# A two-layer hybrid decoder trunk: the first layer's input also given transposed, its first two projections taken over all token blocks at once

## Chip, core and metric

One core of a Trainium2 chip runs the whole program. The metric is the device time of one execution in microseconds (us); lower is better. Engines are named as the profile names them: PE (TensorE matmuls), PEld (its weight loads), DVE (VectorE), ACT (ScalarE), POOL (GpSimd), SP (SyncE, which here only issues DMAs).

## What is computed

A trunk of two layers on 512 tokens of width 2048. Each layer normalises its input, projects it to 5952 columns, runs three groups of attention heads on the result, gates them, projects back and adds the residual. Cut to what bears on the change:

```python
def hybrid_layer(x, cos, sin, layer, pre_w, post_w, w_in, ...):
    h = rms_norm(x, pre_w)
    proj = h @ w_in
    a_q, a_k, a_v, a_g, b_q, b_k, b_v, b_g, c_q, c_kv, c_kr, c_g = jnp.split(proj, offsets, axis=-1)
    ...
    qb = apply_rope(b_q.reshape(B, S, SW_HEADS, SW_HEAD_DIM), cos4, sin4)
    kb = apply_rope(b_k.reshape(B, S, SW_KV_HEADS, SW_HEAD_DIM), cos4, sin4)
    vb = b_v.reshape(B, S, SW_KV_HEADS, SW_HEAD_DIM)
    y_b = sliding_window_attention(qb, kb, vb, sinks)
    ...
    return x + rms_norm(out, post_w)
```

The row scale of the norm, one over the root mean square of a token's row, commutes with the product, so the kernel multiplies the raw `x * pre_w` with `w_in` and puts the row scale on afterwards.

## The kernel before

**Products.** Every float32 operand is split into a rounded high part and a low remainder (`split`, L148: ACT writes the high part, DVE or POOL subtracts it). A product is three matmuls, high by high, high by low, low by high (`three`, L299), so each weight tile passes ACT (`whi`) and then DVE or POOL (`wlo`; even tiles DVE, odd ones POOL). `stream` (L279) loads two weight tiles of 128 rows in one DMA into one of three `raw` buffers; four `whi` and four `wlo` buffers let the splits run at most four tiles ahead of PE. `sweep` (L306) runs over the 16 tiles of a contraction: the first two tiles are taken together, block by block, and so are the last two (`tail=2`). Results lie in four PSUM banks `g`.

**Opening of a layer.** `act_hi` and `act_lo` hold the split input transposed, 16 tiles of 128 rows by 512 tokens. In layer 0 `load` (L1016) fetches `x` in pieces of 128 tokens by 512 columns; `feed` (L510) transposes four 128x128 squares of a piece on PE into a bank `hT`, DVE multiplies it by `pre_norm_w` into `h` (L526), and the split follows. ACT also squares each piece and sums along its row (L540); from these sums `row_scales` makes the row scales `r_in`, and `scaled_tables` (L269) multiplies the rotary tables by them.

The tokens are taken in two halves of two blocks (the loop `for half in range(2)`, L600). Each half sweeps the 320 columns of the keys and values (`C_KR` and `B_K`), then rotates them on DVE (`rope`, L233) into `kd`, then sweeps the 512 columns of the first eight query heads (`B_Q`) and rotates those into `q_rot`. A sweep of two blocks uses two of the four banks, so each weight tile is loaded and split twice, once for either half. `key_half` later transposes `kd` on PE (`kT`). The angle tables of the rotation are computed on DVE at the very start (`rope_tables`, L193), some 40 small instructions.

Then follow sweeps over all 512 tokens: the gates (`gate_chunk`, whose matmuls the rows call `g<-act_hi,whi`, with the activations named first), the other eight query heads, and so on.

**Order.** PE runs in the order in which the program is written. Small pieces of attention work wait in two lanes (`Lanes`), from which `sweep` draws one step after each group of tiles; a step may ask to be left for some microseconds. The other engines' order is set by a scheduler when the program is built; `late` pins an instruction to the written order. Each engine runs its own list strictly in order. SP issues all loads of weights and of `x`.

Of the kernel before, what the change touches and what calls it, by code (L numbers as in the profile page):

```python
# [19 lines left out]
P = 128  # L20
# [88 lines left out]
def trunk(ctx: ExitStack, tc: tile.TileContext, ins, inv_freq, out):  # L109
# [83 lines left out]
    def rope_tables():  # L193
        pos_i = sm("pos_i", NB, I32)
        freq = slot("freq", "et", shape=(P, 32))
        nc.gpsimd.dma_start(out=pos_i, in_=ins["positions"].rearrange("b (m p) -> p (b m)", p=P))
        nc.gpsimd.dma_start(out=freq, in_=inv_freq.partition_broadcast(P))
        co, si = tabs
        pos = sm("pos", NB)
        V.tensor_copy(pos, pos_i)  # L200
        H = 32 * NB
        room = [slot("angles", "rot") for _ in range(2)]
        ang, r, t, *ks = (room[i // 4][:, H * (i % 4):H * (i % 4) + H] for i in range(6))
        for m in range(NB):
            V.tensor_scalar(ang[:, 32 * m:32 * m + 32], freq, pos[:, m:m + 1], None, op0=ALU.mult)
        pc = two_pi_pieces()
        V.tensor_copy(r, ang)
        for k, e in zip(ks, (22, 11, 0)):
            V.tensor_scalar(t, r, 1.0 / (2 * math.pi * 2.0 ** e), MAGIC, op0=ALU.mult, op1=ALU.add)
            V.tensor_scalar(k, t, -MAGIC, None, op0=ALU.add)  # L210
            if e:
                for j in range(3):
                    V.scalar_tensor_tensor(r, k, -pc[j] * 2.0 ** e, r, op0=ALU.mult, op1=ALU.add)
        V.tensor_copy(r, ang)
        for lev, j in ((0, 0), (1, 0), (0, 1), (2, 0), (1, 1), (0, 2), (2, 1), (1, 2), (0, 3), (2, 2)):
            V.scalar_tensor_tensor(r, ks[lev], -pc[j] * 2.0 ** (22, 11, 0)[lev], r,
                                   op0=ALU.mult, op1=ALU.add)
        V.tensor_scalar(t, r, 1.0 / (2 * math.pi), MAGIC, op0=ALU.mult, op1=ALU.add)
# [8 lines left out]
        rv, tv = (z.rearrange("p (m f) -> p m f", f=32) for z in (r, t))  # L227
        A.activation(co[:, :, 0:32], tv, AF.Sin)
# [47 lines left out]

    ahead, behind, fine, last_rows = [False], [True], [False], [False]

    def stream(w, segs, nk, C, rows=0, before=None):  # L279

        for k0 in range(0, nk, 2):
            raw = wraw.tile([P, 2, S], F32, name="raw", tag="raw")
            c = 0
            for off, width in segs:
                nc.sync.dma_start(
                    out=raw[:, :, c:c + width],
                    in_=w[rows + k0 * P:rows + (k0 + 2) * P, off:off + width].rearrange("(k p) c -> p k c", p=P))
# [17 lines left out]

    def sweep(tiles, nk, jobs, after=None, tail=2):  # L306

# [34 lines left out]

    def gemm_tok(block, w, segs, C, nk=KT, ms=range(NB), kruns=None, before=None, tail=2):
# [8 lines left out]
        sweep(tiles(), nk, [lambda t, a, z, p=p, m=m: three(p[:, 0:C], block(t[0], m), t[1:], a, z)  # L352
                            for p, m in zip(ps, ms)], tail=tail)
        return ps
# [112 lines left out]

    def column(name, l, n):

        t = layer_c.tile([P, n], F32, name=f"{name}{l}")  # L470
        if l == 0:
            nc.scalar.dma_start(out=t, in_=ins[name][l].rearrange("(k p) -> p k", p=P))
        else:
            late(nc.sync.dma_start(out=t, in_=ins[name][l].rearrange("(k p) -> p k", p=P)))
        return t

    def layer_constants(l):
        c = dict(qnw=column("mla_q_norm_w", l, 4), kvnw=column("mla_kv_norm_w", l, 4))
        lam_init = 0.8 - 0.6 * math.exp(-0.3 * l)
        sub = layer_c.tile([P, 1], F32, name=f"sub{l}")  # L480
        late(nc.sync.dma_start(out=sub, in_=ins["diff_subln_w"][l].rearrange("(p o) -> p o", o=1)))
        V.tensor_scalar(sub, sub, 0.5 * (1.0 - lam_init), None, op0=ALU.mult)
        sink = layer_c.tile([P, 16], F32, name=f"sink{l}")
# [25 lines left out]

    def feed(half, xs, pre, r_in, there, first=False):  # L510

# [4 lines left out]
        def turn(lane, u):  # L516
            c = slice(u * P, u * P + P)
            for n in range(4):
# [4 lines left out]
                for j in range(4):  # L523
# [4 lines left out]
                                op=ALU.mult)  # L528
                split(act_hi[:, half, 4 * n:4 * n + 4, c], act_lo[:, half, 4 * n:4 * n + 4, c], h,
                      E=nc.gpsimd if first and u else V)  # L530
                done[u] += 1
            yield L_FEED2

        def scale(lane):
            yield L_SCALE
            ssps = [sm("ssp") for _ in range(2)]
            for n in range(4):
                for u in range(2):
                    sq = slot("sq", f"qE{lane}")
                    late(A.activation(sq, xs[n][u], AF.Square, accum_out=ssps[u][:, n:n + 1]), first)  # L540
                yield L_FEED2
# [13 lines left out]
    def layer(l, pre, norms, r_in, start=None):  # L555
# [16 lines left out]
        def fed(half, k):  # L572
            if start and half == 0:
                start(k)
            tasks, done, _ = norms[half]
# [23 lines left out]
        keys = []  # L599
        for half in range(2):  # L600
            ms = (2 * half, 2 * half + 1)
            ps = gemm_tok(act_block, w_in, [(C_KR, 64), (B_K, 256)], 320, ms=ms,
                          before=lambda k: fed(half, k))
            lanes.finish(norms[half][2])
            scaled_tables(r_in, half, rtabs)
            lanes.finish(*keys)
            kd = []
            for t_ps, m in zip(ps, ms):
                d = slot("kd", "rot")
# [5 lines left out]
            keys.append(lanes.add(key_half, half, kd))  # L615
            if half == 0:
                c = layer_constants(l)
            ps = gemm_tok(act_block, w_in, [(B_Q, 512)], 512, ms=ms)
# [32 lines left out]

        def sw_pair(lane, g, pr):
            qq = stack_q(lane, f"qE{lane}", qt[g], 128 * pr)
            yield L_SPLIT
# [301 lines left out]
        post = norm_rows("post_norm_w", l, "k")  # L956
        nxt = None if final else column("pre_norm_w", l + 1, KT)
        ssp = [sm("ssp") for _ in range(NB)]
# [49 lines left out]
    r_in = layer_c.tile([P, NB], F32, name="r_in0")  # L1008
    norms = []

    pre = column("pre_norm_w", 0, KT)
    loads = [(half, n) for half in range(2) for n in range(4)]
    xs = [[[None] * 2 for _ in range(4)] for _ in range(2)]
    there = [[0], [0]]

    def load():  # L1016
        half, n = loads.pop(0)
        for u in range(2):
            m = 2 * half + u
            xs[half][n][u] = slot("x0", "gy")  # L1020
            late(nc.sync.dma_start(out=xs[half][n][u], in_=ins["x"][0, m * P:(m + 1) * P, n * S:(n + 1) * S]))
        there[half][0] += 1
        if n == 0:
            norms.append(feed(half, xs[half], pre, r_in, there[half], half == 0))

    def start(k):
        if loads and k % 2 == 0:
            load()

    rope_tables()  # L1030
    for _ in range(N_LOAD):
        load()
    state = layer(0, pre, norms, r_in, start)
# [13 lines left out]
L_DA = 4.5  # L1047
N_LOAD = 2
L_KEYS = 5.0
# [27 lines left out]
```

## Time and profile before

| | us |
|---|---|
| median of 3 runs | 1787.97 (1786.29 to 1790.8) |
| the profiled execution, its own time | 1790.11 |
| its span in the profile | 1788.3 |
| PE busy in the span | 1732.1 (97%), 8832 matmuls |
| DVE, ACT, POOL busy | 917.7 (51%), 820.1 (46%), 765.6 (43%) |
| DMA | 202.25 MB, mean 113 GB/s |

The profile divides the span into 40 slices of 44.7 us. PE's busy share is six tenths in the first slice, eight in the second and nine or more in nearly all others. A timeline lists instructions by start and duration; matmuls are pipelined, so the time between two starts, and not the duration, is what one costs.

### The profile page before, as it was taken

The page shows a single profiled execution, that of the slowest core. Times are in us where ns is not written, and L with a number is a line of the kernel's source. Part 1 is how long each engine was busy: PE and PEld are TensorE (multiplying, and loading weights), DVE is VectorE, ACT ScalarE, POOL GpSimd, SP SyncE. Part 2 cuts the span into 40 slices and gives each one's busy share as a digit, 9 for nine tenths or more (in the row PEclk, how much of TensorE's full clock was granted, in tenths as well). Part 3 has the DMA queues.
Part 4 walks back from the last instruction along what each step waited for, and adds up shares of the span by engine and source line. Part 5 has one row for each costly group of instructions (what it writes and reads, how often), then busy time and mean ns, then how long its engine had stood idle before and what let it go on. Part 6 is the DMA issues. An engine that isn't in the chain of part 4 may idle for free. (4 is left out here: it accounts for less than half of the span.)

```text
span 1788.3 us, 25313 instructions
## 1 busy us (share of the span) xinstructions
PE 1732.1 (97%) x8832; PEld 1488.4 (83%) x8832; DVE 917.7 (51%) x2246; ACT 820.1 (46%) x1792; POOL 765.6 (43%) x650
## 2 busy tenths in 40 slices
PE   6899999999999999999988999999999999999997
PEld 5778888888899998888777888888889999888885
DVE  7755516654336658301776555256534357672035
ACT  5555525544344545325554454255444444452353
POOL 4343343443434344448344444433434434444550
PEclk9999999999999999999999999999999999999999
DMA  7452232232323233325765422322323222332366
GB/s 196 133 158 77 83 101 83 83 88 78 109 74 84 71 97 110 118 95 186 238 190 151 118 88 83 95 83 67 104 77 104 81 74 75 114 121 96 115 205 221
DMA packets 168671, 202.25 MB, mean 113 GB/s; under 512 B 30800, under 2 KB 92256, under 8 KB 168544
## 3 DMA queue, kind: packets, MB, share of 16 engines
q1 hardware_dynamic: 162160, 190.12, 35.9%
q0 software_dynamic: 3264, 10.51, 1.6%
q8 instruction: 69, 1.13, 0.3%
q10 hardware_dynamic: 3120, 0.01, 0.1%
q14 instruction: 58, 0.48, 0.1%
HBM read 188.02 MB, written 12.58 MB: 112 GB/s over the span
## 5 line engine op out<-in xcount | busy, mean ns | idle before, releaser
L152 POOL TENSOR_TENSOR wlo<-raw,whi 128x512 fp32r<-128x512 f32 (+2 forms) x592 | 734.9, 1248 | 930.2 <-ACT whi L151 899.6
L151 ACT CAST whi<-raw 128x512 fp32r<-128x512 f32 (+3 forms) x704 | 406.0, 581 | 635.4 <-PE g L142 489.5
L142 PE MATMUL g<-wlo,act_hi 128*128 128x512 f32 (+2 forms) x1408 | 522.9, 371 | 26.8 <-DVE wlo L152 23.8
L142 PE MATMUL g<-whi,act_hi 128*128 128x512 f32 (+2 forms) x1408 | 526.9, 374 | 4.1 <-ACT whi L151 4.1
L142 PE MATMUL g<-whi,act_lo 128*128 128x512 f32 (+2 forms) x1408 | 519.5, 369 | 0.6 <-POOL act_lo L152 0.6
L142 PEld LDWEIGHTS g<-wlo,act_hi 128*128 128x128 f32 x1408 | 267.9, 190 | 71.1 <-DVE wlo L152 31.7
L142 PE MATMUL g<-act_hi,whi 128*128 128x512 f32 x768 | 310.9, 405 | 0.6 <-DVE vl L155 0.6
L142 PE MATMUL g<-act_hi,wlo 128*128 128x512 f32 x768 | 303.6, 395 | 0.0
L142 PE MATMUL g<-act_lo,whi 128*128 128x512 f32 x768 | 303.4, 395 | 0.0
L142 PEld LDWEIGHTS g<-whi,act_hi 128*128 128x128 f32 x1408 | 268.0, 190 | 40.0 <-ACT whi L151 5.7
L142 PEld LDWEIGHTS g<-whi,act_lo 128*128 128x128 f32 x1408 | 267.8, 190 | 35.1 <-POOL act_lo L152 0.9
L142 PEld LDWEIGHTS g<-act_hi,wlo 128*128 128x128 f32 x768 | 144.3, 188 | 34.6
L142 PEld LDWEIGHTS g<-act_hi,whi 128*128 128x128 f32 x768 | 144.6, 188 | 30.4 <-DVE vl L155 1.5
L142 PEld LDWEIGHTS g<-act_lo,whi 128*128 128x128 f32 x768 | 144.7, 188 | 29.1
L152 DVE TENSOR_TENSOR wlo<-raw,whi 128x512 fp32r<-128x512 f32 (+1 forms) x112 | 79.0, 711 | 96.0 <-ACT whi L151 95.9
L152 DVE TENSOR_TENSOR pTl<-pT,pTh 128x512 fp32r<-128x512 f32 (+2 forms) x112 | 68.2, 612 | 99.7 <-ACT pTh L151 99.6
L968 DVE TENSOR_TENSOR ob<-g,post_norm_w 128x512 f32<-128x512 f32 x32 | 22.1, 690 | 176.8 <-ACT sq L966 176.7
L151 ACT CAST pTh<-pT 128x512 fp32r<-128x512 f32 (+2 forms) x112 | 58.6, 525 | 45.4 <-PE pT L146 44.6
L436 DVE CUSTOM_DVE_ANT_0 p<-sc,causal 128x128 f32<-128x128 f32 (+3 forms) x96 | 46.0, 480 | 33.1 <-PE sc L142 33.1
L146 PE MATMUL pT<-ident,p 128*128 128x128 f32 x384 | 61.0, 274 | 1.4 <-DVE p L833 1.4
L644 ACT ACTIVATE p<-p,nm 128x256 f32<-128x256 f32 (+1 forms) x128 | 59.9, 469 | 0.0
L438 ACT ACTIVATE p<-p,nm 128x128 f32<-128x128 f32 (+3 forms) x64 | 36.0, 562 | 51.4 <-DVE nm L437 51.4
(236 smaller groups left out, 2042.6 us busy)
## 6 DMA issues: line engine op xcount, KB each, us to landing
raw<-w_in SPq DMA_DIRECT2D x144, 512.0 KB, 3.6
raw<-w_out SPq DMA_DIRECT2D x96, 512.0 KB, 3.8
raw<-w_in SPq DMA_DIRECT2D x192, 128.0 KB, 2.4
raw<-w_in SPq DMA_DIRECT2D x32, 256.0 KB, 3.1
x<-x SPq DMA_DIRECT2D x16, 256.0 KB, 4.8
y_spill<-gate POOLq DMA_DIRECT2D x16, 256.0 KB, 3.0
raw<-w_ukv SPq DMA_DIRECT2D x8, 512.0 KB, 3.8
yb<-y_spill POOLq DMA_DIRECT2D x16, 256.0 KB, 4.0
```

Of the source, the lines that this page charges most:

```text
L142: nc.tensor.matmul(out_, a, b, start=start, stop=stop, skip_group_check=True)
L146: nc.tensor.transpose(out_, in_, ident)
L151: late(A.copy(hi, src), behind)
L152: E.tensor_tensor(lo, src, hi.bitcast(F32), op=ALU.subtract)
L436: V.tensor_tensor_reduce(p, scores, mask, 1.0, -3e38, op0=ALU.add, op1=ALU.max, accum_out=mx)
L438: A.activation(p, p, AF.Exp, bias=nm, scale=scale, accum_out=den)
L644: A.activation(blocks[i], blocks[i], AF.Exp, bias=nm[:, i:i + 1], scale=64.0 ** -0.5, accum_out=den[:, i:i + 1])
L968: V.tensor_tensor(ob[n][m], t, post[n], op=ALU.mult)
```

## The change

The host writes two more inputs: `x_t`, the transposed input as 16 tiles of 128 rows by 512 tokens, and `cols`, the per-column norm weights with one row of 25 numbers per partition (before, they were fetched as single numbers by several DMAs). In layer 0:

- there are no transposes and no `hT`, `h`: `take` splits a tile of `x_t` straight into `act_hi` and `act_lo`, with `pre_norm_w` as the scale of both instructions;
- the squares are taken of the transposed tiles (`square`), added tile by tile on DVE into `ssum`, and PE sums over the partitions (`col_sums`, tile `css`) in a lane task, `first_scale`, which is added at step 13 of the first sweep;
- the first sweep is the queries' (512 columns) for all four blocks, without the pairing of its first two tiles (`head=False`); the scaled tables and the rotation of the four query blocks follow; the second sweep is the keys' and values' (320 columns) for all four blocks, with `tail=3`;
- `rope_tables` is cut into pieces that are written between the steps of the first sweep;
- the very first weight load is two DMAs of one tile each; the residual is still read from `x`.

Layer 1 keeps its halves; only its column weights come from `cols`.

```diff
-            if n == 0 or nk - tail <= n < nk - 1:
+            if (n == 0 and head) or nk - tail <= n < nk - 1:
...
+        kv_segs = [(C_KR, 64), (B_K, 256)]
+        if start:
+            ps = gemm_tok(act_block, w_in, [(B_Q, 512)], 512, before=start, head=False)
+            lanes.finish(*norms)
+            for half in range(2):
+                scaled_tables(r_in, half, rtabs)
+            for m in range(NB):
+                qt[0][m] = rotate_q(ps[m], m)
+            c = layer_constants(l, pre)
+            kd = key_tiles(gemm_tok(act_block, w_in, kv_segs, 320, tail=3), range(NB), None)
+            keys += [lanes.add(key_half, half, kd[2 * half:2 * half + 2]) for half in range(2)]
+        for half in range(0 if start else 2):
...
+    def take(k):
+        x = xt[k].rearrange("p (h t) -> p h t", h=2)
+        split(act_hi[:, :, k, :], act_lo[:, :, k, :], x, pre[:, k:k + 1], behind=k < 4)
...
+        late(A.activation(sq, xt[k], AF.Square))
+        if k:
+            V.tensor_tensor(ssum, ssum, sq, op=ALU.add)
+        if k == KT - 1:
+            norms.append(lanes.add(first_scale))
+
+    def first_scale(lane):
+        yield L_FIRST
+        ms = sm("ms")
+        V.tensor_scalar(ms, col_sums(bank("css", lane), ssum), 1.0 / DM, EPS, op0=ALU.mult, op1=ALU.add)
+        V.tensor_copy(r_in, rsqrt(ms, "rin"))
+        yield 0.0
...
+    def start(k):
+        while loaded[0] < min(2 * k + 3, k + N_LOAD, KT):
+            load(loaded[0])
+            loaded[0] += 1
+        while taken[0] < min(k + 1 if k < 2 else 2 * k, k + N_TAKE, KT):
+            take(taken[0])
+            taken[0] += 1
+        for _ in range(2):
+            if squared[0] < min(2 * (k - 3), taken[0]):
+                square()
...
+N_LOAD = 6
+N_TAKE = 3
+L_FIRST = 2.0
```

**PE, from the first sweep to the second, in the changed kernel.** `g_135` is the fourth bank of the queries' sweep, `g_632` the first of the keys'; the two share no name but the pool has four banks, so `g_632` takes the place of the queries' first bank.

```order
L142 MATMUL g_135<-whi_534,act_hi_88 128x512
L142 MATMUL g_135<-wlo_535,act_hi_88 128x512
L142 MATMUL g_135<-whi_534,act_lo_89 128x512
L142 MATMUL css_563<-ones_f_91,ssum_115 128x2 x4
L142 MATMUL g_632<-whi_639,act_hi_88 128x320
L142 MATMUL g_632<-wlo_640,act_hi_88 128x320
```

The sums `css` stand behind the last matmul of the queries' sweep and right ahead of the keys' first one; before, the row sums came from ACT, and PE had no part in them.

**DVE at the same place in the changed kernel** (`ms` is the mean square, `rsq_u` and `rin` the steps of its inverse root, `rcos` and `rsin` the scaled tables, L249 to L259 the rotation).

```order
L1058 TENSOR_SCALAR ms<-css 128x4
L160 TENSOR_SCALAR rsq_u<-ms 128x4
...
L1059 COPY r_in_112<-rin 128x4
L281 TENSOR_TENSOR rcos<-cos,r_in_112 128x128
...
L249 TENSOR_TENSOR rope<-g,rsin 128x8x32
L251 TENSOR_TENSOR rope<-g,rsin 128x8x32
L253 TENSOR_TENSOR q_rot<-g,rcos 128x512
L249 TENSOR_TENSOR rope<-g,rsin 128x8x32
L259 TENSOR_TENSOR q_rot<-q_rot,rope 128x512
```

From `ms` to `r_in` stand 13 instructions, then four of the tables, then four rotations of four instructions each, with the fourth of a rotation one place later, behind the first of the next.

**DVE within the first sweep, before:**

```order
L526 TENSOR_TENSOR h_269<-hT_264,pre_norm_w0_113 128x512
L213 SCALAR_TENSOR_TENSOR angles_121<-angles_122,angles_121 128x128
L526 TENSOR_TENSOR h_278<-hT_273,pre_norm_w0_113 128x512
L209 TENSOR_SCALAR angles_121<-angles_121 128x128
L526 TENSOR_TENSOR h_297<-hT_292,pre_norm_w0_113 128x512
```

**and in the change:**

```order
L219 SCALAR_TENSOR_TENSOR angles_169<-angles_169 128x128
L152 TENSOR_TENSOR wlo_397<-raw_380,whi_396 128x512
L219 SCALAR_TENSOR_TENSOR angles_169<-angles_170,angles_169 128x128
L155 SCALAR_TENSOR_TENSOR act_lo_89<-xt_313,cols0_113,act_hi_88 128x2x256
L219 SCALAR_TENSOR_TENSOR angles_169<-angles_170,angles_169 128x128
L1051 TENSOR_TENSOR ssum_115<-ssum_115,sq_416 128x512
```

Ahead of `ms` DVE now has 16 instructions on `act_lo`, 15 on `ssum`, 8 on the queries' `wlo` and about 42 small ones, mixed like this; the `h` instructions, which read PSUM, are gone.

## Rows read from the trace of the kernel before

Rows of stretches give the stretch and its length, then busy time and number of instructions of PE, PEld, DVE, ACT and POOL, then the granted clock, the DMA share and GB/s. Rows of a timeline give start, duration, engine, line, operation and tiles.

**Rows 1.** Busy time by engine in one stretch, the opening up to the gates:

```profile
0.00:115.00 115.00, 92.34 (x462) 78.06 (x463) 78.73 (x189) 62.98 (x140) 48.15 (x53) 0.96 0.61 171
```

**Rows 2.** What PE waited for in the first 115 us (total, times, longest):

```profile
PE g L142 <- DVE wlo L152: 12.9, 8, 5.5
```

**Rows 3.** Timeline of PE, steady matmuls of both widths, and the gates' first:

```profile
84.75 0.31 PE L142 MATMUL g<-wlo,act_hi 128*128 128x320 f32 x1
...
89.73 0.31 PE L142 MATMUL g<-whi,act_lo 128*128 128x320 f32 x1
...
104.72 0.40 PE L142 MATMUL g<-whi,act_lo 128*128 128x512 f32 x1
...
114.52 0.40 PE L142 MATMUL g<-whi,act_lo 128*128 128x512 f32 x1
114.75 0.40 PE L142 MATMUL g<-act_hi,whi 128*128 128x512 f32 x1
```

**Rows 4.** Timeline of PE after its longest wait in the opening:

```profile
28.41 0.64 PE L142 MATMUL g<-wlo,act_hi 128*128 128x320 f32 x1 [5.54 <-DVE wlo L152]
28.85 0.47 PE L142 MATMUL g<-whi,act_lo 128*128 128x320 f32 x1
29.12 0.47 PE L142 MATMUL g<-whi,act_hi 128*128 128x320 f32 x1
...
32.58 0.40 PE L142 MATMUL g<-wlo,act_hi 128*128 128x320 f32 x1
```

**Rows 5.** Timeline of the first 10 us: loads of x, first transposes, first product:

```profile
0.74 1.81 SPq L1021 DMA_DIRECT2D x<-x  x4
...
4.28 1.09 PE L146 MATMUL hT<-ident,x 128*128 128x128 f32 x4 [4.28 <-DMA x<-x]
...
10.07 0.64 PE L142 MATMUL g<-whi,act_hi 128*128 128x320 f32 x1 [3.01 <-ACT whi L151]
```

**Rows 6.** Busy time in two stretches of 5 us, for the DMA rate (last column):

```profile
0.00:5.00 5.00, 0.72 (x4) 0.72 (x4) 0.00 (x0) 0.37 (x1) 3.59 (x14) 1.00 0.56 105
...
15.00:20.00 5.00, 5.00 (x39) 4.86 (x37) 4.28 (x12) 2.37 (x6) 1.47 (x2) 1.00 1.08 363
```

**Rows 7.** Timeline of DVE: small and wide passes, each with its successor:

```profile
28.29 0.28 DVE L216 SCALAR_TENSOR_TENSOR angles<-angles 128x128 f32<-128x128 f32 x1
28.49 0.48 DVE L152 TENSOR_TENSOR wlo<-raw,whi 128x320 fp32r<-128x320 f32 x1
...
43.38 0.68 DVE L152 TENSOR_TENSOR act_lo<-h,act_hi 128x512 fp32r<-128x512 f32 x1
43.98 0.15 DVE L165 SCALAR_TENSOR_TENSOR rin<-rsq_u,rin 128x2 f32<-128x2 f32 x1
```

**Rows 8.** Timeline of POOL and DVE side by side:

```profile
24.08 2.13 POOL L152 TENSOR_TENSOR wlo<-raw,whi 128x320 fp32r<-128x320 f32 x2
24.13 1.36 DVE L152 TENSOR_TENSOR act_lo<-h,act_hi 128x512 fp32r<-128x512 f32 x1
...
52.32 1.29 POOL L152 TENSOR_TENSOR wlo<-raw,whi 128x512 fp32r<-128x512 f32 x1 [3.91 <-ACT whi L151]
```

**Rows 9.** Timeline: column sums on PE and the inverse root on DVE, later in layer 0:

```profile
378.97 0.95 PE L142 MATMUL css<-ones_f,ssum 128*128 128x2 f32 x8
...
379.96 0.16 DVE L739 TENSOR_TENSOR ms<-css,r_sq 128x4 f32<-128x4 f32 x1 [9.22 <-PE css L142]
...
382.54 0.16 DVE L741 SCALAR_TENSOR_TENSOR qscale<-rlat,r_in 128x4 f32<-128x4 f32 x1
```

**Rows 10.** Timeline of DVE: a scaled table, and the rotation of one query block:

```profile
46.01 0.28 DVE L274 TENSOR_TENSOR rcos<-cos,r_in 128x128 f32<-128x128 f32 x1
...
71.98 0.41 DVE L242 TENSOR_TENSOR rope<-g,rsin 128x256 f32<-128x256 f32 x1
72.31 0.41 DVE L244 TENSOR_TENSOR rope<-g,rsin 128x256 f32<-128x256 f32 x1
72.64 0.68 DVE L246 TENSOR_TENSOR q_rot<-g,rcos 128x512 f32<-128x512 f32 x1
```

More of the change, by code (lines that the diff above doesn't have):

```diff
@@ L274, in scaled_tables @@
             V.tensor_tensor(dst[:, mm_, :], src[:, mm_, :], rb, op=ALU.mult)
-    ahead, behind, fine, last_rows = [False], [True], [False], [False]
+    ahead, behind, fine, last_rows, opening = [False], [True], [False], [False], [True]
     def stream(w, segs, nk, C, rows=0, before=None):
@@ L284, in stream @@
             for off, width in segs:
-                nc.sync.dma_start(
-                    out=raw[:, :, c:c + width],
-                    in_=w[rows + k0 * P:rows + (k0 + 2) * P, off:off + width].rearrange("(k p) c -> p k c", p=P))
+                for j, n in ((0, 1), (1, 1)) if opening[0] else ((0, 2),):
+                    nc.sync.dma_start(
+                        out=raw[:, j:j + n, c:c + width],
+                        in_=w[rows + (k0 + j) * P:rows + (k0 + j + n) * P, off:off + width].rearrange(
+                            "(k p) c -> p k c", p=P))
+                opening[0] = False
                 c += width
@@ L304, in three, with sweep @@
         mm(out_ap, al, bh, start=False, stop=last)
-    def sweep(tiles, nk, jobs, after=None, tail=2):
+    def sweep(tiles, nk, jobs, after=None, tail=2, head=True):
         def run(group):
@@ L341, in gbanks, with gemm_tok @@
         return [psg.tile([P, S], F32, name="g", tag="g") for _ in range(n)]
-    def gemm_tok(block, w, segs, C, nk=KT, ms=range(NB), kruns=None, before=None, tail=2):
+    def gemm_tok(block, w, segs, C, nk=KT, ms=range(NB), kruns=None, before=None, tail=2, head=True):
         ps = gbanks(len(ms))
@@ L465, in spread, with columns, layer_constants @@
         mm(t, ones_r, diag[1], start=False, stop=True)
[L468 to L474, printed above, removed]
[L475 to L478 removed]
+    def columns(l):
+        t = layer_c.tile([P, KT + 9], F32, name=f"cols{l}")
+        late((nc.sync if l else nc.scalar).dma_start(out=t, in_=ins["cols"][l]), l > 0)
+        return t
+    def layer_constants(l, cols):
+        c = dict(qnw=cols[:, KT:KT + 4], kvnw=cols[:, KT + 4:KT + 8])
         lam_init = 0.8 - 0.6 * math.exp(-0.3 * l)
         sub = layer_c.tile([P, 1], F32, name=f"sub{l}")
[L481 to L482 removed]
+        V.tensor_scalar(sub, cols[:, KT + 8:KT + 9], 0.5 * (1.0 - lam_init), None, op0=ALU.mult)
         sink = layer_c.tile([P, 16], F32, name=f"sink{l}")
@@ L508, in row_scales, with feed @@
         return rsqrt(ss, name, n)
-    def feed(half, xs, pre, r_in, there, first=False):
+    def feed(half, xs, pre, r_in, there):
         done = [0, 0]
@@ L528, in turn @@
                                 op=ALU.mult)
-                split(act_hi[:, half, 4 * n:4 * n + 4, c], act_lo[:, half, 4 * n:4 * n + 4, c], h,
-                      E=nc.gpsimd if first and u else V)
+                split(act_hi[:, half, 4 * n:4 * n + 4, c], act_lo[:, half, 4 * n:4 * n + 4, c], h)
                 done[u] += 1
@@ L599, in layer, with key_tiles @@
         keys = []
[L600 to L606, printed above, removed]
+        def key_tiles(ps, ms, tag):
             kd = []
             for t_ps, m in zip(ps, ms):
-                d = slot("kd", "rot")
+                d = slot("kd", tag or f"p{m % 2}")
                 rope(d[:, 0:384], t_ps[:, 0:192], m, 3, rtabs, dup=3)
@@ L614, in layer @@
                           r_in[:, m:m + 1])
-            keys.append(lanes.add(key_half, half, kd))
+            return kd
+        kv_segs = [(C_KR, 64), (B_K, 256)]
[10 more added lines that the diff above has]
+        for half in range(0 if start else 2):
+            ms = (2 * half, 2 * half + 1)
+            ps = gemm_tok(act_block, w_in, kv_segs, 320, ms=ms, before=lambda k: fed(half, k))
+            lanes.finish(norms[half][2])
+            scaled_tables(r_in, half, rtabs)
+            lanes.finish(*keys)
+            keys.append(lanes.add(key_half, half, key_tiles(ps, ms, "rot")))
             if half == 0:
-                c = layer_constants(l)
+                c = layer_constants(l, pre)
             ps = gemm_tok(act_block, w_in, [(B_Q, 512)], 512, ms=ms)
@@ L652, in sw_pair @@
         def sw_pair(lane, g, pr):
+            if not all(t["done"] for t in keys):
+                yield lambda: all(t["done"] for t in keys)
             qq = stack_q(lane, f"qE{lane}", qt[g], 128 * pr)
@@ L956, in layer @@
         post = norm_rows("post_norm_w", l, "k")
-        nxt = None if final else column("pre_norm_w", l + 1, KT)
+        nxt = None if final else columns(l + 1)
         ssp = [sm("ssp") for _ in range(NB)]
@@ L1009, in trunk, with load, square @@
     norms = []
[L1011 to L1024, printed above, removed]
-    def start(k):
[L1027 to L1032, printed above, removed]
+    pre = columns(0)
+    xt, ssum = [None] * KT, slot("ssum", "raw")
+    pieces = rope_tables()
+    def load(k):
+        xt[k] = slot("xt", "gy")
+        late(nc.sync.dma_start(out=xt[k], in_=ins["x_t"][:, k, :]))
+    def take(k):
+        x = xt[k].rearrange("p (h t) -> p h t", h=2)
+        split(act_hi[:, :, k, :], act_lo[:, :, k, :], x, pre[:, k:k + 1], behind=k < 4)
+    loaded, taken, squared = [1], [0], [0]
+    def square():
+        k = squared[0]
+        squared[0] += 1
+        sq = slot("sq", f"qE{k % 2}") if k else ssum
+        late(A.activation(sq, xt[k], AF.Square))
[9 more added lines that the diff above has]
+        yield 0.0
+    def start(k):
+        while loaded[0] < min(2 * k + 3, k + N_LOAD, KT):
[7 more added lines that the diff above has]
+                square()
+        behind[0] = k < 3
+        if k:
+            next(pieces, None)
+    next(pieces)
+    load(0)
     state = layer(0, pre, norms, r_in, start)
@@ L1047 @@
 L_DA = 4.5
-N_LOAD = 2
+N_LOAD = 6
+N_TAKE = 3
+L_FIRST = 2.0
 L_KEYS = 5.0
```

20 lines of the change are left out of this document (16 added, 4 removed).

## The prediction

> **What bounds the kernel now.** The page comes first: PE is busy 97% of the span, the other engines about half of it, so PE's own order sets the time, except where PE waits. Next come the stretches. The opening, up to the gates' first matmul at 114.75 us [rows 3], holds only 92.3 us of busy PE in 115 [rows 1]; nearly all that this change can reach lies there. Then the waits of PE: the largest is for DVE's low parts of the weights, 12.9 us in 8 times, one of them 5.5 us [rows 2]. DVE is the busiest of the helpers there, 78.7 us [rows 1], so the opening is bound by DVE in its first part and by PE in its last.
>
> What PE must do in the opening is small. From 84.75 to 89.73 us lie 34 steps between matmuls of 320 columns, 0.1465 us each; from 104.72 to 114.52 lie 42 of 512 columns, 0.2333 us each [rows 3]. The two projections are 4 blocks by 16 tiles by 3, 192 matmuls of either width: 44.8 us for the queries and 28.1 us for the keys and values, 72.9 us of 114.75. The rest is transposes, waits, and a slow clock.
>
> **What the change removes.** 64 transposes leave PE. The sixteen wide `h` passes leave DVE. Every weight tile of the two projections is split once instead of twice, so 32 of 64 splits go. Fifteen wide `ssum` sums and the 13 instructions of one inverse root come instead of two such chains. I build the new opening as a sum of clock times and compare its end, the gates' first matmul, with 114.75.
>
> **1. First matmul: 6.3 us.** The first piece of `x` is there at 4.28 [rows 5]; the first tile of `x_t` is as large and first in SP's queue. Then a high part, the weights' high part and a low part follow one another, each a wide pass of 0.6 to 0.7 us [rows 7]: 4.28 + 3 x 0.65 = 6.2, taken as 6.3. Bounds: 4.9 (one pass, the rest beside it) and 10.07, where the first product starts now [rows 5].
>
> **2. Slow clock at the start: 2.3 us.** PE after its long idle ran a 320-column step in 0.27 us instead of 0.1465, from 28.41 to 32.58 us, 4.2 us long [rows 4]; that is the 1.2 GHz level beside the 2.4 GHz one. At 6.3 us PE has done nothing, so the first 12 matmuls of 512 columns cost about 0.427 each instead of 0.233: 12 x 0.194 = 2.3 us. Bounds 0 and 4.6, twice that.
>
> **3. The queries' sweep: 44.8 us, and 1.6 us of waits.** DVE has to keep pace. Until the last low part of this sweep it has 39 wide passes (16 `act_lo`, 15 `ssum`, 8 `wlo`), a wide pass releasing its successor after 0.60 us, and about 42 small ones at 0.2 us [rows 7], 0.22 with their dependences: 23.4 + 9.2 = 32.6 us, less than PE's 44.8. But a wide DVE pass with both operands in SBUF, started beside a POOL subtraction, took 1.36 us instead of 0.68 [rows 8]. POOL has 8 subtractions of 512 columns here, 1.29 us each [rows 8]; they would add 10.3 us to DVE if each blocked it in full: 42.9. It starts at about 5 and waits some 2 us for its first tiles, so it ends at 49.9; PE needs that low part two tiles (24 matmuls, 5.6 us) ahead of its own end at 6.3 + 2.3 + 44.8 = 53.4, at 47.8. The wait is thus 0 to 2.1 us; 1.6 is taken, since nearly every wide pass now has both operands in SBUF. The sweep ends at 55.0. The Trainium skill, "SBUF — State Buffer", section "Who interferes with whom", says that a VectorE instruction with two SBUF inputs and a GpSimd one that reads SBUF exclude each other for a whole instruction. The trace agrees (1.36 for 0.68). By that rule in its full form the wait is 2.1 us and the time 0.5 us longer; without it, 0 and 1.6 us shorter.
>
> **4. From the queries to the keys: 9.3 us lost.** This is what the change adds. All four banks hold query results, and PE's next matmul needs the first of them. `css` stands behind the sweep's last matmul, so the whole chain to the row scale starts there. PE's sums to `ms`: 378.97 to 379.96, 1.0 us; from `ms` over 13 steps to the last: 2.6 us [rows 9]. Four table products, started every 0.2 us, by their 0.28 us duration: 0.9 [rows 7, 10]. The first block's three PSUM reads start 0.33 and 0.33 apart and the third, a wide pass, frees the bank 0.60 after its start [rows 7]: 1.26 [rows 10]. With 0.4 for a POOL subtraction in the way [rows 8], PE goes on 1.0 + 2.6 + 0.9 + 1.3 + 0.4 = 6.2 us after the sweep. Each later block costs DVE four instructions, 0.33 + 0.33 + 0.60 + 0.60 = 1.86 us, so the fourth bank is free at 6.2 + 5.6 = 11.8. Between them PE has six matmuls a block, 0.9 us at full clock and 1.6 at half, which [rows 4] an idle time of 6 us brings; both fit into 1.86. After the last six, at 12.8, PE has done 24 matmuls worth 3.5: 9.3 us lost. Bounds: 7 (tables and POOL beside the chain) and 13 (slow clock for 4 us afterwards, and every DVE pass held up).
>
> **5. The keys' sweep: 28.1 us.** Its splits take half the columns per PE time of before and DVE has little else. **6. On to the gates: 0.3 us.** The keys' rotation reads at most 320 columns of a bank, so no block costs more than 1.86 us against 1.3 us (9 x 0.1465) of PE's last group per block; at the most 4 x 0.56 = 2.2 us. **7. Later: 1.2 us.** The 12 transposes of the keys, before within the opening, now come among the gates' matmuls, at under the 0.1465 of a 320-column step: at most 1.8, taken as 1.2.
>
> Sum: 6.3 + 2.3 + 44.8 + 1.6 + 9.3 + 28.1 + 0.3 + 1.2 = 93.9 us against 114.75: **20.8 us saved**. Behind it PE runs without a gap, so the start of all that follows moves by as much. The single tidier column loads of layer 1 I cost at nothing: SP has slack there, and if it had none they would be worth under 1 us. The profiled execution took 1790.11, which is 2.1 above the median of 1787.97; 1790.11 - 20.8 = 1769.3, against the median 1767.2 us.
>
> **Rivals.** (a) *DVE bounds the opening.* If the POOL exclusion also lengthens POOL, whose delayed odd tiles hold PE, and each small step waits for its predecessor, DVE gets 39 x 0.68 + 42 x 0.32 + 10.3 = 50.3 us instead of 42.9: 7.4 us more before the first matmul of the last group, most of it PE's. Saved 13 to 14, 1774 us. For it: DVE bounds the opening now [rows 2]. Against: the small steps are mixed with wide ones, which hides their dependences. (b) *The gain is given back.* The keys are transposed later, so the sliding-window tasks in the lanes start later; if their first four had to be waited for, PE would idle. It would end within 5 us of 1788. Against: in the order their last matmuls still stand 12 tiles of 12 matmuls ahead of the point that needs them (20 before), 12 x 12 x 0.233 = 33 us. (c) *Slower: the loads starve the opening.* The first sweep needs 4.2 MB of `x_t` and 4.2 MB of weights within the first 50 us. At 105 GB/s, as in the first 5 us, 8.4 MB take 80 us, the sweep ends at about 82, and the opening takes 121 us: 1794 us. It decides below 8.4 MB in 55 + 20.8 = 76 us, 111 GB/s. Against: 363 GB/s flowed from 15 to 20 us [rows 6], in the same 2 KB lines. (d) *The clock stays low.* The four short bursts of step 4 are too thin to bring the clock back, and the keys' sweep runs its first 4.2 us at half speed, as after the 5.5 us gap [rows 4]: 2.1 us more, with the last burst's 0.7 some 2.8, 1770 us. For it: PE is busy 4 x 0.9 of 12.8 us. Against: at half clock the bursts last 1.6 of each 1.86 us, nearly without a gap. The Trainium skill, "TensorE: Matmul & The Clock Gate", section "HAM oscillation — how this bites in real kernels", describes PE falling back to the cold clock in each of many waits; that speaks for (d), and the trace shows it for one long gap (0.27 us for 0.1465).
>
> **How the numbers follow.** About 0.3%, 5.4 us, is what a measurement of this kernel can tell from no change. The forecast, the sum of the steps, has 0.63, (a) 0.24, (b) 0.05, (c) 0.03, (d) 0.05. The forecast alone spans 1761 to 1772: the favourable bounds (first matmul 1.4 earlier, no DVE wait, 7 instead of 9.3) save 26 us, the unfavourable ones (3.7 later by step 4, some more cold clock) 16. (d) lies inside it, and with (a) the range reaches 1776. Faster by over 0.3%: 0.91, which leaves a little of (a) aside; the same 0.06; slower 0.03.
>
> **What would show it.** Right: the first matmul near 6 us; no `hT`; css near 55; then PE waiting about 6 us for DVE, four short bursts, and the gates' first matmul at 91 to 95 us; everything behind it shifted alike. Wrong: waits for `wlo` spread over the first sweep (a), SP's loads landing after their tile is due (c), or new PE waits between 150 and 250 us (b).

## The result, and the profile after

The changed kernel took **1767.11 us**, the median of 4 runs (1766.71 to 1769.09), against 1788.34 for the kernel before in 4 runs beside them: ratio 0.9883, 95% interval 0.9866 to 0.9900. Its profiled execution took 1767.51 us, with a span of 1765.7 (before: 1790.11 and 1788.3).

| place in the program (us from the span's start) | before | after | earlier by |
|---|---|---|---|
| first product | 10.07 | 6.44 | 3.6 |
| gates' first matmul, layer 0 | 114.75 | 92.10 | 22.7 |
| first transpose of `da_q` | 540.5 | 521.3 | 19.2 |
| layer 1: first `hT` | 855.9 | 836.8 | 19.1 |
| layer 1: last `kT` of `kd` | 982.1 | 959.7 | 22.4 |
| end of the span | 1788.3 | 1765.7 | 22.6 |

First the opening by engine, up to the gates' first matmul (columns as in [rows 1]), and then three stretches of 5 us around the place where the queries' sweep ends:

```profile
0.00:92.30 92.30, 79.14 (x393) 68.30 (x394) 60.28 (x147) 42.65 (x79) 26.65 (x32) 0.96 0.45 139
...
55.00:60.00 5.00, 0.68 (x7) 0.59 (x6) 4.05 (x20) 0.45 (x1) 0.86 (x1) 0.85 0.25 66
60.00:65.00 5.00, 4.08 (x13) 3.53 (x14) 5.00 (x12) 0.00 (x0) 0.00 (x0) 0.50 0.01 2
65.00:70.00 5.00, 4.56 (x30) 4.33 (x30) 3.71 (x13) 1.48 (x4) 0.91 (x1) 0.97 0.11 27
```

Against [rows 1], up to the same place, PE is busy 13 us less and DVE 18 us less. What PE waited for in the first 115 us, all of it:

```profile
PE g L142 <- ACT whi L151: 6.4, 1, 6.4
PE g L142 <- DVE q_rot L253: 5.2, 1, 5.2
PE g L142 <- DVE wlo L152: 1.0, 1, 1.0
PE g L142 <- DVE rh L463: 0.4, 1, 0.4
PE g L142 <- DVE vb L155: 0.4, 1, 0.4
```

The 12.9 us for `wlo` [rows 2] have become one wait of 1.0, and a wait of 5.2 us for the rotation of the queries has come instead. Both, the two stretches at half clock and the gates' first matmul stand in PE's timeline:

```profile
6.44 0.79 PE L142 MATMUL g<-whi,act_hi 128*128 128x512 f32 x1 [6.44 <-ACT whi L151]
7.32 0.79 PE L142 MATMUL g<-wlo,act_hi 128*128 128x512 f32 x1
...
10.47 0.50 PE L142 MATMUL g<-whi,act_lo 128*128 128x512 f32 x1
10.81 0.39 PE L142 MATMUL g<-whi,act_hi 128*128 128x512 f32 x1
...
11.51 0.39 PE L142 MATMUL g<-whi,act_hi 128*128 128x512 f32 x1
...
32.47 0.50 PE L142 MATMUL g<-wlo,act_hi 128*128 128x512 f32 x1 [0.96 <-DVE wlo L152]
...
54.73 0.95 PE L142 MATMUL css<-ones_f,ssum 128*128 128x2 f32 x8
...
60.91 0.60 PE L142 MATMUL g<-whi,act_hi 128*128 128x320 f32 x1 [5.23 <-DVE q_rot L253]
...
62.78 0.61 PE L142 MATMUL g<-whi,act_hi 128*128 128x320 f32 x1
...
65.31 0.31 PE L142 MATMUL g<-whi,act_lo 128*128 128x320 f32 x1
...
66.50 0.39 PE L142 MATMUL g<-whi,act_hi 128*128 128x320 f32 x1 [0.44 <-DVE rh L463]
...
67.46 0.31 PE L142 MATMUL g<-whi,act_hi 128*128 128x320 f32 x1
...
92.10 0.39 PE L142 MATMUL g<-act_hi,whi 128*128 128x512 f32 x1
```

In the second slow stretch the granted clock is 0.50, the lower of its two levels (1.2 for 2.4 GHz). For the first, before 10.81, that column reads 1.00 throughout; there the half rate is read from the steps alone (0.43 us for 0.233).

The bursts start at 60.91, 62.78, 64.64 and 66.50, a pitch of 1.86 us. DVE shows the chain that PE waits for in its 5.2 us: sums, twelve steps, tables, first block.

```profile
55.72 0.16 DVE L1058 TENSOR_SCALAR ms<-css 128x4 f32<-128x4 f32 x1 [0.50 <-PE css L142]
...
58.41 0.17 DVE L1059 COPY r_in<-rin 128x4 f32<-128x4 f32 x1
58.61 0.29 DVE L281 TENSOR_TENSOR rcos<-cos,r_in 128x128 f32<-128x128 f32 x1
...
59.43 0.42 DVE L249 TENSOR_TENSOR rope<-g,rsin 128x256 f32<-128x256 f32 x1
59.76 0.41 DVE L251 TENSOR_TENSOR rope<-g,rsin 128x256 f32<-128x256 f32 x1
60.09 0.68 DVE L253 TENSOR_TENSOR q_rot<-g,rcos 128x512 f32<-128x512 f32 x1
```

### The profile page after: what moved, and what is told of

It is laid out like the page before. It is cut to its first block, busy times and chain, and to the rows that moved or that the text cites. A ratio compares the mean times of both kernels' runs of the same rounds, so it can differ in the third digit from the quotient of the medians.

```text
span 1765.7 us, 24988 instructions
## 1 busy us (share of the span) xinstructions
PE 1719.0 (97%) x8776; PEld 1478.0 (84%) x8776; DVE 899.5 (51%) x2216; ACT 803.5 (46%) x1744; POOL 746.6 (42%) x630
## 5 line engine op out<-in xcount | busy, mean ns | idle before, releaser
L152 POOL TENSOR_TENSOR wlo<-raw,whi 128x512 fp32r<-128x512 f32 (+3 forms) x576 | 721.9, 1261 | 932.3 <-ACT whi L151 905.0
L151 ACT CAST whi<-raw 128x512 fp32r<-128x512 f32 (+2 forms) x672 | 388.9, 583 | 626.5 <-PE g L142 481.4
L152 DVE TENSOR_TENSOR wlo<-raw,whi 128x512 fp32r<-128x512 f32 (+1 forms) x96 | 66.2, 695 | 90.1 <-ACT whi L151 90.0
```

Of the source, the lines that this page charges most:

```text
L151: late(A.copy(hi, src), behind)
L152: E.tensor_tensor(lo, src, hi.bitcast(F32), op=ALU.subtract)
```

## The experiments

The "gates" below are the gates' first matmul in layer 0, 92.10 us in the changed kernel.

**Sums asked for earlier.** In `first_scale` of the changed kernel:

```
-        yield L_FIRST
```

> The changed kernel with one line taken out, the lane task's first pause, so that PE's column sums stand behind step 13 of the queries' sweep and no longer behind its last matmul. Theory (the chain from the sums to the first rotated block, 6.2 us, is what PE waits for between the sweeps): the chain then lies beside the last two steps, PE starts the keys within 1 us of the queries' end, the first group of the keys' sweep ends about 7 us earlier, and the kernel takes about 1760 us. Rival (the four rotations set the pace, and the chain is hidden by them): the first group ends at most 1 us earlier, 1766 to 1767 us.

Measured: 1763.45 us (1761.79 to 1765.50), ratio 0.9862 (0.9848 to 0.9877); gates at 87.27. The sums run at 49.87, two tiles (24 matmuls) before the sweep's end, and the wait of 5.2 us has become three short ones:

```profile
PE g L142 <- DVE q_rot L253: 2.0, 3, 0.7
...
49.87 0.95 PE L142 MATMUL css<-ones_f,ssum 128*128 128x2 f32 x8
...
57.95 0.39 PE L142 MATMUL g<-whi,act_hi 128*128 128x320 f32 x1 [0.54 <-DVE q_rot L253]
```

The chain was the wait, and it can be covered. The gates came 4.8 us earlier, not 7: the four bursts still start at DVE's pitch of 1.86 us while each holds 0.9 us of products, which costs 2.7, and the queries' sweep ended 1.6 us later (56.36 for 54.73), half of that by the sums, which now stand inside it. Of the 4.8 us the median shows 3.7. By all its runs, none over 1765.50 where the changed kernel had none under 1766.71, this version beats both kernels.

**Layer 1's columns loaded singly.** `column(...)` of the kernel before again for layer 1, the packed columns for layer 0 only.

> The changed kernel, but layer 1 fetches its four column weights again singly, by four DMAs of single numbers on SP's queue, as the kernel before does. Theory of the prediction (SP has slack there): at most 1 us slower than the changed kernel, 1767 to 1768 us. Rival (these DMAs stand ahead of weight loads in layer 1's opening and hold PE): 2.5 to 3.5 us slower, about 1770 us, and PE's waits in layer 1's opening are those of the kernel before.

Measured: 1766.7 us, ratio 0.9886 (0.9873 to 0.9898). Layer 1's opening, first `hT` to last `kT`, took 123.8 us against 122.9 in the changed kernel, a difference within what this stretch varies by in one and the same kernel (122.6 and 126.2, below). No cost of the single loads shows.

**The packed columns alone,** in the kernel before:

```
-    pre = column("pre_norm_w", 0, KT)
+    pre = columns(0)
```

> The kernel before with nothing but the packed column weights, one DMA per layer, in place of the single ones. Theory of the prediction: at most 1 us faster than before, 1787 to 1788 us. Rival (the single-number DMAs hold up weight loads): 2.5 to 3.5 us faster through layer 1's opening, and up to 3 more where they also hold up the first loads of layer 0: 1782 to 1786 us.

Measured: 1785.35 us in 12 runs (1781.33 to 1788.26), ratio 0.9985 (0.9977 to 0.9994); gates at 110.84 instead of 114.75, layer 1's opening 122.8. That is the rival's time, but not its place: it expected the larger part of the gain in layer 1's opening, which is as long as in the second profile of the kernel before (122.6, below). What came earlier is layer 0's opening, where issuing three column loads kept ACT busy until 4.6 us and issuing one keeps it until 1.1; that this is the reason is not shown. By the medians some 2.3 us of the change's 21 come from this alone, though in the changed opening they need not add up the same way.

**The transposed input without the new order:** the changed kernel with the loop over halves back, each half keys first, then queries.

> The changed kernel with the transposed input, but layer 0 projects in two halves again, keys before queries, with weights loaded and split twice. Theory (the gain needs a first sweep that is long enough on PE to cover DVE's 43 us of low parts, squares and angles): the first sweep, 14 us on PE, is stretched to about 48 us by DVE, the three others (59 us) follow without a gap, the gates start near 108 to 110 us and the kernel takes about 1782 to 1785 us. Rival (the transposes and the PSUM passes were what cost, and the order of the sweeps matters little): the gates start near 95 us, about 1770 us.

Measured: 1786.7 us, ratio 0.9993 (0.9985 to 1.0002); gates at 113.48. What PE waited for in its first 115 us:

```profile
PE g L142 <- DVE wlo L152: 12.2, 10, 3.1
PE g L142 <- ACT whi L151: 10.5, 4, 6.4
```

Without the transposes and the `h` passes, and still no measurable gain: the first narrow sweep, over half the blocks, lasts from 6.42 to 45.94 us for 14.1 us of products, with 10.2 us of the waits for `wlo` in it: it cannot cover what DVE does beside it. That is the theory's mechanism; gates and time lie 3.5 and 1.7 us beyond its ranges, since the three other sweeps took 67.5 us to the gates and not 59.

**Keys and values first,** all blocks at once:

```
-            ps = gemm_tok(act_block, w_in, [(B_Q, 512)], 512, before=start, head=False)
+            ps = gemm_tok(act_block, w_in, kv_segs, 320, before=start, head=False)
...
-            kd = key_tiles(gemm_tok(act_block, w_in, kv_segs, 320, tail=3), range(NB), None)
+            kd = key_tiles(ps, range(NB), None)
+            ps = gemm_tok(act_block, w_in, [(B_Q, 512)], 512, tail=3)
```

> The changed kernel with the two sweeps exchanged: keys and values for all four blocks first, while x^T is split, then the queries for all four. TensorE's own work is the same. Theory (step 3: the first sweep is free of waits because four blocks of 512 columns, 44.8 us of products, are longer than the some 43 us of splits, squares and tables that VectorE does beside them): keys and values are only 28 us of products, so VectorE sets the first sweep's end at about 45 to 50 us instead of 34.5, with 10 to 15 us of waits for wlo; the gates' first product comes at 102 to 107 instead of 92.1, and the time is 1777 to 1782. Rival (all blocks at once is what pays, in whichever order): the waits stay under 3 us, gates at 92 to 95, time within 3 us of 1767.

Measured: 1776.08 us (1775.32 to 1778.53), gates at 103.11. The first sweep began at 6.99 and ended at 47.27, where its products alone (28.1 us) would have ended at 35. Only 6.2 of these 12 us are listed as waits for `wlo` and `whi` after the start; the rest lies in the slower steps around each wait and at half clock. The wait behind the sweep grew from 5.2 to 7.2. Of the 11.0 us by which the gates come later than in the changed kernel, 8.7 are lost within the first sweep and 1.9 behind it. The direction and place hold: it matters that the *wide* sweep runs while `x_t` is split. About 9 of the 21 us hang on that order.

**TensorE busy before the first product.**

```
+    wt = bank("css", 0)
+    for _ in range(28):
+        transpose(wt[:, 0:P], ident)
```

> The changed kernel with 28 transposes of the identity on TensorE before the first product (the identity is written by 1.76 us, the first product waits until 6.44). Theory (step 2: the first twelve products ran at the lower clock level because TensorE had done nothing before them, 0.427 us a step instead of 0.233, until 10.47): with TensorE busy from about 2 us on, the steps run at 0.233 us from the start, the first sweep's end comes from 54.73 to about 52.7, and the median falls by 1.5 to 2 us to about 1765. Rival (the early products are paced by the first loads and splits of ACT and VectorE, the clock only shows beside them): the products start warm but wait, the sweep's end moves by less than 0.5 us and the time stays at 1767. A third way: transposes of 128 columns do not raise the clock; then the first steps stay at 0.43 us.

Measured: 1772.83 us, slower than the changed kernel by 5.7; gates at 96.04. The first products did run at full clock:

```profile
1.82 5.32 PE L146 MATMUL css<-ident 128*128 128x128 f32 x28 [1.82 <-POOL ident masks.py:199]
...
7.71 0.40 PE L142 MATMUL g<-whi,act_hi 128*128 128x512 f32 x1
7.95 0.39 PE L142 MATMUL g<-wlo,act_hi 128*128 128x512 f32 x1
...
21.15 0.50 PE L142 MATMUL g<-wlo,act_hi 128*128 128x512 f32 x1 [1.45 <-DVE wlo L152]
```

Twelve steps took 2.92 us instead of 5.07, so the transposes did bring up the rate, and the third way is out. The first product stood behind them until 6.90 instead of 6.44, and after its twelve steps PE was 1.7 us ahead. Five waits for `wlo`, 4.3 us as listed and some 6 with the slower steps around them, put the column sums at 58.28 instead of 54.73. Theory and rival both missed.

**The same without the additions of squares,** so that DVE has 10 us less to do, first without the transposes and then with them:

```
-        if k:
-            V.tensor_tensor(ssum, ssum, sq, op=ALU.add)
```

> The changed kernel without the 15 additions of the squares on VectorE (the row sums then hold the squares of the first 128 features alone; 15 times 0.68, 10.2 us less for VectorE in the first sweep). It is the pair to the next run. Theory (TensorE and VectorE stand level in the first sweep, and TensorE sets its end by little): the one wait of 0.96 us goes, column sums at 53.6 to 53.9 instead of 54.73, median 1765.5 to 1767. Rival (VectorE sets the sweep's end): sums 2 us earlier or more, time under 1765.

> The same without the additions, and with the 28 transposes ahead of the first product. With VectorE's additions in place the warm start lost 4 to 5 us. Theory (it lost them because VectorE, level with TensorE, could not follow a TensorE that starts 2 us ahead): with 10 us less on VectorE the waits for wlo stay under 1 us, the first sweep ends 1.5 to 2 us before that of the run without the transposes (51.7 to 52.3), and the median is 1.5 to 2.5 us below it. Rival (the transposes themselves do harm, by the order that the scheduler builds from them): waits of 3 us or more again, the sweep ends no earlier, the time is equal or worse.

Measured: without the transposes 1766.22 us, sums at 53.73, one wait of 0.2 for `wlo`; TensorE alone sets that sweep's end, as the theory had it. With them 1772.28, waits of 3.1, sums at 56.62: the rival. DVE's load is not what the warm start lost to. ACT's timelines of the two runs show what moved: the splits (`whi`) of the fifth, seventh and ninth weight tiles. First without the transposes (the first line holds the fifth and sixth):

```profile
16.96 1.13 ACT L151 CAST whi<-raw 128x512 fp32r<-128x512 f32 x2
...
20.27 0.61 ACT L151 CAST whi<-raw 128x512 fp32r<-128x512 f32 x1
...
24.02 0.61 ACT L151 CAST whi<-raw 128x512 fp32r<-128x512 f32 x1
```

And with them:

```profile
18.36 0.60 ACT L151 CAST whi<-raw 128x512 fp32r<-128x512 f32 x1
...
23.85 0.61 ACT L151 CAST whi<-raw 128x512 fp32r<-128x512 f32 x1
...
32.51 0.60 ACT L151 CAST whi<-raw 128x512 fp32r<-128x512 f32 x1
```

PE waits for `wlo` at just these tiles, 1.17, 0.81 and 0.68 us. At the fifth PE came 1.1 us earlier than in the partner run, while DVE's low part came 0.4 later (19.95 for 19.53). The partner run waits 0.2 us there itself, so the helpers had no slack for a head start. At the seventh and ninth the splits themselves came 3.6 and 8.5 us later. The two kernels differ by the 28 transposes alone, so these changed the order of ACT and DVE, which a scheduler sets when the program is built; by which reckoning it did so is not shown, nor how much of the loss the order makes. Whether a warm start pays with the old order was not tried.

**The splits put ahead,** early sums and transposes kept (`tc.high_priority()` around the splits of the first sweep).

> The run with early sums, with the 28 transposes ahead of the first product, and with the splits of the weights and of x^T in the first sweep put ahead of the squares' sums and the tables wherever they are ready. It asks what ate the gain of the warm start in the run before (first product at full clock, yet 4.3 us of waits for wlo and the sweep's end 3.5 us later). Theory: VectorE takes its work in order, and sums and tables stood ahead of the splits at the moment TensorE, 2 us earlier, asked for them; with the splits first the waits fall under 1.5 us, the first sweep ends at 52 to 53.5, the gates' first product comes at 85 to 86.5 (87.3 with early sums alone) and the median is 1761 to 1763. Rival: VectorE's whole work in this sweep (some 43 us beside 44.8 of products) is the limit, in whatever order; then 3 us of waits or more remain, the gates come at 88 or later and the time is 1765 to 1770.

Measured: 1769.09 us, gates at 93.00: the rival's numbers, yet not by its mechanism. One wait of 4.9 us at 24.34 makes most of the 6.0, and before it DVE stood idle 0.8 and 1.3 us for the loads of `positions` and `inv_freq`, which the priorities had pushed behind a subtraction on POOL (issued at 10.94 and 12.82 instead of 2.22 and 3.62). The question of the order stays open by this run.

**A longer first group in the keys' sweep** (`head`, now a number, holds four tiles), first with the transposes and early sums:

> A version meant to be shorter than both: the column sums asked for three tiles before the first sweep's end, the 28 transposes ahead of the first product, and the first group of the keys' sweep four tiles long instead of two, so that each block's burst (1.76 us at full clock) is as long as the rotation of a block's queries on VectorE (1.86 us). Theory: 2 us from the warm start and about 2 more at the restart, beside the run with early sums alone: gates' first product at 83 to 84 (87.3 there, 92.1 in the changed kernel), median 1758.5 to 1761. Rival (what is gained at the restart is lost to the splits of tiles 2 and 3, which then stand among the rotations on VectorE): gates at 85.5 to 87, median 1761.5 to 1763.5.

Measured: 1769.81 us, gates at 93.67, both expectations missed, and of PE's 8.7 us of waits for `wlo` one of 4.4 is of the rival's kind. DVE reached the low part of the group's third tile only behind all but the last of the sixteen rotation passes:

```profile
63.87 0.68 DVE L253 TENSOR_TENSOR q_rot<-g,rcos 128x512 f32<-128x512 f32 x1
64.47 0.48 DVE L152 TENSOR_TENSOR wlo<-raw,whi 128x320 fp32r<-128x320 f32 x1
...
65.00 0.63 PE L142 MATMUL g<-wlo,act_hi 128*128 128x320 f32 x1 [4.43 <-DVE wlo L152]
```

Then without the transposes, and with the low parts of tiles 2 and 3 on POOL:

> The run with early sums, with the first group of the keys' sweep four tiles long, and the low parts of tiles 2 and 3 on GpSimd, where they do not stand behind the rotations (in the run with the long group VectorE reached tile 2's low part only at 64.47, after seven of the eight rotation steps, and TensorE waited 4.4 us for it). Theory: the bursts of 1.76 us keep pace with the rotations' 1.86, TensorE waits under 1 us there instead of 2.0, gates at 85.5 to 86.5 (87.3 with early sums alone), median 1761 to 1763. Rival: GpSimd's subtractions hold up rotation steps on VectorE (1.3 us a piece, as in [rows 8]), the group ends no earlier, gates at 87 or later, median 1763 to 1766.

Measured: 1764.63 us (1762.10 to 1765.62), gates at 88.45. The bursts no longer wait; the fifth tile's `wlo` does, 2.5 us at 66.01. It does not stand behind the rotations, which end by 61.6, but behind what follows them on DVE: an idle time of 1.7 us for a load of small constants (`lam_in`), and two passes held up beside POOL's subtractions.

```profile
60.89 0.68 DVE L259 TENSOR_TENSOR q_rot<-q_rot,rope 128x512 f32<-128x512 f32 x1
63.29 0.79 DVE L498 TENSOR_TENSOR lam_j<-lam_in 128x64 f32<-128x64 f32 x1 [1.72 <-DMA lam_in<-diff_lambda_k]
...
64.08 1.35 DVE L468 TENSOR_TENSOR dh<-ident,rh 128x512 fp32r<-128x512 f32 x1
...
65.48 0.48 DVE L152 TENSOR_TENSOR wlo<-raw,whi 128x320 fp32r<-128x320 f32 x1
```

The high part of that tile was there by 62.6. So the gain at the bursts was lost to the order of DVE's list, and by its time this is no better than early sums alone; what the longer group is worth with that tile's `wlo` ahead of the `lam_in` passes was not tried.

**The kernel before once more.**

> The kernel before once more, unchanged, for a second profile of it. In the first profile layer 1's opening (first transpose of x to the last of the keys) took 126.2 us, in the changed kernel's 122.9, and the prediction had nothing there. If that stretch varies by itself from run to run (theory), it is now 122.5 to 126.5 and need not be 126.2; if the changed kernel saves there, it is again over 125.8. Span 1785 to 1789.

Measured: span 1785.1. Its landmarks in layer 1 (first and last start in us, after the durations):

```profile
L146 PE MATMUL hT<-ident,ob x64: 270/272/299, 856.3 to 944.5; 128*128 128x128 f32 x64
...
L146 PE MATMUL kT<-ident,kd x24: 270/272/273, 67.5 to 978.9; 128*128 128x128 f32 x24
```

978.9 less 856.3 is 122.6 us, where the first profile of the same kernel had 126.2. The 3.3 us that layer 1 seemed to save between the profiles of before and after belong to that one profile.

## Why the prediction was right

Predicted 1767.2, measured 1767.11. Step by step:

- **1, first matmul 6.3:** 6.44, by luck: two errors in the terms cancel. The tile of `x_t` was there at 3.86, not 4.28, and the first matmul waited for two passes, not three, since it needs no low part; but ACT first spent 1.28 us on loading a table, which the step did not have, though the kernel before shows one too, at 4.63. In the run with the packed columns alone it stands at 1.18, before any data is there; here it began only when the tile had come.

```profile
3.86 1.28 ACT L154 ACT_TABLE_LOAD   x1 [3.86 <-DMA xt<-x_t]
5.16 0.72 ACT L154 ACTIVATE act_hi<-xt,cols 128x512 fp32r<-128x512 f32 x1
5.78 0.60 ACT L151 CAST whi<-raw 128x512 fp32r<-128x512 f32 x1
```

- **2, slow clock 2.3:** the first twelve steps took 5.07 us for 2.80 at full rate, 2.3 lost. But only nine of them were slow, some 1.7 us, and 0.6 is the wait for the first `wlo` at 7.32 with the step behind it. The size held, its make-up did not. That it could be had back by a busy PE did not follow from it: two pairs of runs that differ in the transposes alone were slower with them, by 5.7 and 6.1 us.
- **3, waits of 1.6 in the queries' sweep:** one, listed with 0.96 us and worth 1.2 between the starts around it, with the sweep's end at 54.73 for 55.0. It did not come about as the step has it. There DVE's list as a whole ends too late for the last low part; in fact DVE began that one at 46.74 and PE wanted it at 49.4. The wait came from one collision in mid-sweep:

```profile
29.84 1.82 POOL L152 TENSOR_TENSOR wlo<-raw,whi 128x512 fp32r<-128x512 f32 x1 [5.82 <-ACT whi L151]
30.43 1.38 DVE L219 SCALAR_TENSOR_TENSOR angles<-angles 128x128 f32<-128x128 f32 x1
31.73 0.68 DVE L152 TENSOR_TENSOR wlo<-raw,whi 128x512 fp32r<-128x512 f32 x1
```

The pass L219 beside POOL's subtraction took 1.38 us instead of 0.28, just ahead of the `wlo` that PE wanted. Only seven DVE passes before 48 us were held up so, and TensorE set the sweep's end: with 10 us less on DVE it came 1.0 us earlier. So the exclusion that the step names is in the trace, and that the size is near is luck.
- **4, restart 6.2 and 12.8 after the sweep:** 6.18 and 12.73, and here the parts hold as well: sums to `ms` 1.0 (1.0 predicted), from `ms` to the tables 2.9, with 0.3 of it beside a POOL subtraction (2.6 and 0.4), tables 0.8 (0.9), first block to PE's start 1.5 (1.3). The half clock of the bursts cost nothing of its own: a burst of 1.6 us ends before the next bank is free, and with early sums the bursts kept the pitch of 1.86 us at full clock. The early sums show that all but the rotations' pitch can be covered.
- **5 and 6:** from the end of the bursts to the gates 24.64 us, as 28.1 less the 3.5 already done; gates at 92.10, predicted 92.7. The drain of the banks came after the gates' first matmul instead of before it.
- **7, later 1.2:** its own term is right, but it leaves out most of what was lost behind the gates. Between the gates and `da_q` the shift falls from 22.65 to 19.2, 3.45 us. The twelve transposes of the keys at 104.56 cost 1.3 of it between starts, as predicted. Another 1.3 is the drain of the banks between 93 and 97 us, which step 6 had at 0.3, and 0.6 is a wait for the gate that was not there before; the rest is spread. Steps 6 and 7 together were 2 us too small; steps 1 to 6 up to the gates were 0.6 too long.
- **The single number is closer than its parts,** and that is luck. The sum of the steps is 20.8 us; the shift that both profiles of the kernel before share is 19.2 at `da_q` and 19.4 at the end (1785.1 less 1765.7); the medians differ by 21.2 against the four runs beside it and by 20.5 against the 1787.65 of 23 runs. Some 1 to 2 us between profile and medians stay unexplained. Layer 1's columns at nothing: no cost shows.
- **Rivals:** (a), DVE as the bound, shows only in the variants: with halves, with keys first. Its condition held in part: POOL was held up too, its eight subtractions in this sweep took 1.28 to 3.50 us and 14.6 together for 10.3, but PE never waited for one. (b) 3.45 us came back, not 20. (c) the loads ran at up to 397 GB/s from 10 to 15 us, and after the first product no wait for a load stands in PE's list. (d) the clock was back by 65.3, ahead of the last burst.

## What to carry to other kernels

Put the widest matmul sweep where the helpers have most to do: the narrow sweep first cost 9 us with all blocks (1776.08), and narrow sweeps over halves first, which also split every weight twice, nearly the whole gain (1786.7). When a sweep takes all banks, look at the chain that frees the first one, and start its sums before the sweep's last tiles. An edit that gives PE a head start may lose more than it gives: the helpers may have no slack where PE now comes earlier, and a scheduler may order them anew. Both were seen here, the share of either was not. Read the order of the helpers before believing the price of such an edit.

## What was not expected of the hardware

- Small passes on DVE are held up as long as wide ones. Beside a subtraction on POOL the pass L219 of 128 columns took 1.38 us instead of 0.28, L212 took 1.32 at 22.79 instead of 0.21, and the cast L201 of four columns 1.28 at 13.15 (0.17 in the kernel before); the wide L155 took 1.78 instead of 0.74. Each cost 1.0 to 1.1 us more, somewhat less than a POOL pass (1.29), whatever its own length. The prediction had priced it for wide passes only, though the trace of the kernel before has a copy of 128 columns at 22.92 that took 1.29. The Trainium skill, "SBUF — State Buffer", section "Who interferes with whom", names casts and `tensor_scalar`, under conditions on their operands, besides passes with two SBUF inputs; the trace agrees, with the 1.28 and the 1.32.
- Short gaps did not keep the clock low. From 60.91 on PE worked through bursts at 0.267 us a step with gaps of about 0.13 us between them, and from 65.31 on at 0.1465. After the first bursts in the run with early sums, gaps of 0.5 and 0.7 us left it at the full rate (granted clock 1.00 from 56.4 to 62.6). In the run with keys first a wait of 2.4 us was followed by the lower rate: PE resumed at 30.40, ran seven steps at the full rate and then, from 31.56 to 34.76, at 0.267 us a step (granted clock 0.50).
